# Values of two heads in one product of 512 columns, and a new order of heads and projections

## The chip, the core and the metric

The kernel runs on one core of one Trainium2 chip. The metric is the device time of one execution in microseconds. The kernel before took 1372.91 us (median of three runs, 1370.94 to 1373.17).

A core has TensorE (PE in the profile, with the loads of its stationary operand shown apart as PEld), VectorE (DVE), ScalarE (ACT) and GpSimd (POOL). SyncE (SP) and POOL issue the DMAs here. Each engine executes its own instructions in the order in which they were issued to it, and waits at an instruction until what that instruction needs is there. TensorE multiplies into PSUM, which has eight banks of 128 x 512 float32. VectorE and ScalarE read and write PSUM and SBUF.

## The reference

One decoder layer on 1024 tokens of 1024 features, all in float32. The part that the change touches is the retention mixer:

```python
h = rmsnorm(x, ln_mix)
z = h @ w_in                       # q | k | v | gate | pool | branch gates
qh = rotary(q) * dk ** -0.5        # 4 heads of 128
kh = rotary(k)
vh = v                             # 4 heads of 256
ret = retention_chunkwise(qh, kh, vh)
```

`retention_chunkwise` cuts the tokens into eight chunks of 128. In each chunk and head it takes decayed scores of q and k times v, and adds q times a running state. The state is 128 x 256 per head and goes from chunk to chunk: decay times the state before, plus k transposed times v of the chunk. After it come a norm per head, a gate, an output projection, a pooling mixer, gated mixing, and an MLP with squared relu. The result must agree with this in float32, so each matrix operand is carried as a pair of reduced-precision parts, an upper and a lower, and each product is three: upper by upper, upper by lower, lower by upper (`PASSES`).

## The kernel before

Activations lie feature-major in `hT[k][half]`: for each of eight blocks k of 128 features and each half of 512 tokens, a tile with the upper and the lower part. The stages follow one another: load and scale x, retention by heads, the pool input (`pool_input`, tiles `pu` and `u`), blocks for a Strassen-like scheme (`mixed_blocks`, tiles `xw` and `hx`), twelve mixer units (`ps_Xmx` and so on), output projections, and the MLP.

In the retention stage `rotary` makes q or k of a head: 24 products of 512 columns for each half of the tokens (the weight is stationary, `hT` moves), then four VectorE steps. `values(h)` makes v of one head, tokens by features: `hT` is stationary (128 tokens), and the weight of the head moves with its 256 columns, 24 products for each of eight token tiles; two token tiles share a PSUM bank. v is split into upper and lower parts (`split_scaled`, ScalarE and then VectorE) and stays in SBUF until `retain(h)`.

`retain(h)` is a chain over all four engines. Keys are transposed (`ps_kt`), scaled and split (`kz`). Scores (`ps_s`) are masked in place and split (`scm`). q is split (`qp`). For each chunk `ps_kv` is k times v, `st` the new state (a VectorE step that reads the state before), and `sp` its split. `ps_ret` adds scores times v and q times state. Then `rn` is copied, its statistics taken (`bst`, `mv`, `rs`, `nb`), and normalised. `transposed` turns it (`ps_rt`), and `retn` goes to DRAM.

PSUM has two pools: five banks "mm" for projections and values, three banks "aux" for `retain` and `transposed`. SBUF tiles are rings by tag. The tag "raw" has two buffers of 4 KB a partition: `load_raw` loads each 512 KB piece of a weight into one, and the piece is split into a `w_` tile from there. A new user of a buffer waits until the one before has been read.

The kernel is written stage by stage, but a scheduler sets the order on each engine when the program is built. It goes by its own estimates of durations, prefers what was written earlier, and puts an instruction where it believes that its inputs are ready; work written later fills the gaps of a chain. On the chip that order is fixed.

## Time and profile before

| | before |
|---|---|
| time, median of three runs | 1372.91 us |
| profiled execution | 1370.83 us, span 1369.0 us |
| granted TensorE clock, mean | 0.997 |
| TensorE busy | 1353.6 us, 99% of the span |
| VectorE, ScalarE busy | 987.9 us (72%), 565.1 us (41%) |
| value products | 41.7 to 224.6 us of the span, 768 of 256 columns |
| first mixer unit's first product | 285.07 us |

A row of the profile names the line of the kernel, engine, operation, tile written and tiles read, the shape, the count, busy time and mean duration, and the idle time of the engine just before with what ended it. Matmuls are pipelined: the duration of one is longer than the distance to the next, and the pace is read from starts. A window row gives the stretch in us, its length, busy us and count of instructions of each engine, and at its end the granted TensorE clock, the DMA share and GB/s; a window with a filter counts only the instructions that the filter leaves. In the list of DMA issues stand the bytes of one transfer and the median time from its issue to its landing.

### The profile page before, as it was taken

How to read it: one execution, taken by the hardware profiler on the slowest of the kernel's cores; microseconds unless marked ns; L12 is line 12 of the kernel's file. 1: busy time of each engine (PE TensorE's matmuls, PEld its weight loads, DVE VectorE, ACT ScalarE, POOL GpSimd, SP SyncE). 2: the span in 40 equal slices, each digit the busy share in tenths (PEclk: the TensorE clock that was granted, in tenths of full speed). 3: DMA queues.
4: the chain of work that ended last, by engine and by line, in shares of the span. 5: the costliest groups of instructions: out<-in, count | busy, mean ns of one | idle time of the engine just before them, and what ended most of it. 6: DMA issues, size and time to landing. Idle time of an engine off the chain costs nothing. (4 is left out here: it accounts for less than half of the span.)

```text
span 1369.0 us, 17491 instructions
## 1 busy us (share of the span) xinstructions
PE 1353.6 (99%) x6572; PEld 1138.6 (83%) x6572; DVE 987.9 (72%) x1631; ACT 565.1 (41%) x960; POOL 86.1 (6%) x151
## 2 busy tenths in 40 slices
PE   9999999999999999999999999999999999999997
PEld 6998999878888888888887888888888888888886
DVE  5766565789966768628657878777787977689665
ACT  6234425463334344113445433333333544444372
POOL 0000001111000000000001011101111000000000
PEclk9999999999999999999999999999999999999999
DMA  9122021354342367124422344433437989778423
GB/s 360 50 62 77 17 92 63 124 215 158 121 172 85 112 238 261 62 77 170 154 77 77 116 169 169 151 126 147 169 139 292 407 330 351 261 266 307 159 70 123
DMA packets 65444, 225.07 MB, mean 164 GB/s; under 512 B 7376, under 2 KB 9424, under 8 KB 61264
## 3 DMA queue, kind: packets, MB, share of 16 engines
q1 hardware_dynamic: 47152, 158.66, 32.7%
q0 software_dynamic: 17920, 65.02, 12.5%
q8 instruction: 51, 0.84, 0.3%
q10 hardware_dynamic: 288, 0.29, 0.1%
q14 instruction: 33, 0.27, 0.1%
HBM read 167.31 MB, written 56.62 MB: 164 GB/s over the span
## 5 line engine op out<-in xcount | busy, mean ns | idle before, releaser
L121 PE MATMUL ps_v<-w_v_hi,hT 128*128 128x256 f32 x512 | 96.0, 284 | 0.0
L199 PE MATMUL ps_Xup<-mv,w_up 128*128 128x512 f32 x384 | 93.0, 390 | 1.7 <-DVE w_up L135 1.7
L199 PE MATMUL ps_Zup<-mv,w_up 128*128 128x512 f32 x384 | 92.5, 389 | 0.8 <-ACT w_up L134 0.8
L853 PE MATMUL ps_dnX<-db,da 128*128 128x512 f32 x384 | 93.1, 389 | 0.1
L134 ACT ACTIVATE w_up<-raw_up 128x512 fp32r<-128x512 f32 x96 | 58.3, 627 | 84.4 <-DVE raw_up L192 46.3
L199 PE MATMUL ps_Vup<-mv,w_up 128*128 128x512 f32 x384 | 92.6, 389 | 0.0
L121 PE MATMUL ps_yr<-retT,w_ret 128*128 128x512 f32 x384 | 88.5, 389 | 0.5 <-ACT w_ret L94 0.5
L121 PE MATMUL ps_o<-mixT,w_o 128*128 128x512 f32 x384 | 87.5, 389 | 0.0
L199 PEld LDWEIGHTS ps_Xup<-mv,w_up 128*128 128x128 f32 x384 | 71.9, 188 | 16.9 <-DVE w_up L135 2.1
L121 PEld LDWEIGHTS ps_yr<-retT,w_ret 128*128 128x128 f32 x384 | 72.0, 188 | 15.8 <-ACT w_ret L94 0.9
L199 PEld LDWEIGHTS ps_Zup<-mv,w_up 128*128 128x128 f32 x384 | 72.0, 188 | 15.7 <-ACT w_up L134 0.8
L853 PEld LDWEIGHTS ps_dnX<-db,da 128*128 128x128 f32 x384 | 72.0, 188 | 15.5 <-DVE db L135 0.5
L199 PEld LDWEIGHTS ps_Vup<-mv,w_up 128*128 128x128 f32 x384 | 72.0, 188 | 15.1 <-ACT w_up L134 0.2
L121 PEld LDWEIGHTS ps_o<-mixT,w_o 128*128 128x128 f32 x384 | 72.0, 188 | 15.0
L135 DVE TENSOR_TENSOR w_up<-raw_up,w_up 128x512 fp32r<-128x512 f32 x96 | 64.2, 685 | 26.4 <-ACT w_up L134 26.1
L121 PEld LDWEIGHTS ps_v<-w_v_hi,hT 128*128 128x128 f32 x512 | 80.8, 192 | 0.0
L134 ACT ACTIVATE w_mx<-raw_mx 128x512 fp32r<-128x512 f32 x72 | 43.6, 626 | 86.0 <-DVE raw_mx L192 44.0
L121 PE MATMUL ps_v<-w_v_lo,hT 128*128 128x256 f32 x256 | 72.6, 284 | 0.0
L199 PE MATMUL ps_Xmx<-hT,w_mx 128*128 128x512 f32 x288 | 72.0, 396 | 0.3 <-ACT w_mx L134 0.3
L199 PE MATMUL ps_Vmx<-hx,w_mx 128*128 128x512 f32 x288 | 69.5, 389 | 0.0
L728 ACT ACTIVATE act<-act 128x512 f32<-128x512 f32 x64 | 40.3, 629 | 65.6 <-DVE act L727 62.2
L199 PEld LDWEIGHTS ps_Xmx<-hT,w_mx 128*128 128x128 f32 x288 | 55.1, 192 | 12.5 <-ACT w_mx L134 0.6
(249 smaller groups left out, 2819.9 us busy)
## 6 DMA issues: line engine op xcount, KB each, us to landing
act_dram<-act POOLq DMA_DIRECT2D x48, 512.0 KB, 4.7
ad<-act_dram SPq DMA_DIRECT2D x48, 512.0 KB, 6.6
raw_up<-in_w_up_dram SPq DMA_DIRECT2D x16, 1024.0 KB, 5.0
raw_mx<-in_w_mix_dram SPq DMA_DIRECT2D x12, 1024.0 KB, 6.2
sg_dram<-mx POOLq DMA_DIRECT2D x16, 512.0 KB, 4.7
wa_lo<-in_w_down_dram SPq DMA_DIRECT2D x16, 512.0 KB, 9.0
wb_hi<-in_w_down_dram SPq DMA_DIRECT2D x16, 512.0 KB, 7.5
wc_lo<-in_w_down_dram SPq DMA_DIRECT2D x16, 512.0 KB, 4.3
```

The costliest lines, as they stand in the source:

```text
L121: nc.tensor.matmul(ps, stationary(k, sa), moving(k, sb), start=i == 0, stop=i == n - 1)
L134: nc.scalar.activation(dst[:, 0, :], src, AF.Copy)
L135: nc.vector.tensor_tensor(dst[:, 1, :], src, dst[:, 0, :].bitcast(F32), ALU.subtract)
L199: nc.tensor.matmul(ps, ws[x][:, sa, k * P : (k + 1) * P], moving[x][k][:, sb, :], start=start and k == 0 and n == 0, stop=k == 3 and n == ...
L728: nc.scalar.activation(dst, dst, AF.Square)
L853: nc.tensor.matmul(banks[i][:, c0 : c0 + n], w[:, sa, i * P : (i + 1) * P], x[:, sb, c0 : c0 + n], start=start and j == 0 and m == 0, stop ...
```

## The change

`values` now makes two heads at once: the moving operand is 512 columns wide, 256 of head h and 256 of head h + 1, and each token tile fills one PSUM bank. The weight of a pair comes in four pieces of 512 KB (`value_weights`): two are split into `w_` tiles, two into four tiles of the tag "a".

In the first call (heads 0 and 1) the values of head 0 are split as before; those of head 1 are scaled by ScalarE into a tile `vf` of the tag "raw" and written to DRAM by the POOL queue. In the second call (heads 2 and 3) both heads go to DRAM that way. `stored_values(h)` loads them back (`vs`) and splits them. The three heads' values are written and read once, 1 MB each way per head.

The order in which the work is written changes too: the second call's weights are asked for before `retain(0)`, its products come after head 1's `retain` and `transposed`, q and k of head 2 follow these, and q and k of head 3 come after head 2's. Nothing else is computed differently.

```diff
-    def load_wide(src, name, raws=None):
-        whi, wlo = w_tile(name + "_hi"), w_tile(name + "_lo")
-        for i in range(2):
-            sl = slice(i * S, (i + 1) * S)
-            raw = raws[i] if raws else load_raw(src[i], f"{name}_{i}")
-            split_weights(raw, whi[:, sl], wlo[:, sl])
-        return [w.rearrange("p (k j) -> p k j", j=256) for w in (whi, wlo)]
...
-    raw_v = [load_raw(a["w_v"][0][0], "w_v0_0")]
-    raw_v.append(load_raw(a["w_v"][0][1], "w_v0_1"))
+    raw_v = [load_raw(a["w_v"][0][i], f"w_v0_{i}") for i in range(4)]
...
-    def values(h):
-        w = load_wide(a["w_v"][h], f"w_v{h}", raw_v if h == 0 else None)
+    v_dram = dram_tile("v_dram", (NH, P, TT, DV))
+
+    def value_weights(h, raws=None):
+        ws = []
+        for i in range(4):
+            raw = raws[i] if raws else load_raw(a["w_v"][h // 2][i], f"w_v{h}_{i}")
+            if i < 2:
+                w = w_tile(f"w_v{h}_{i}").rearrange("p (s n) -> p s n", s=2)
+                split_weights(raw, w[:, 0, :], w[:, 1, :])
+                ws += [w[:, :, :HALF], w[:, :, HALF:]]
+            else:
+                for j in range(2):
+                    w = pair_tile("a", f"w_v{h}_{i}_{j}")
+                    split_pair(w, raw[:, j * HALF : (j + 1) * HALF])
+                    ws.append(w)
+        return ws
+
+    def values(h, ws, direct=None):
+
+        for t in range(TT):
+            half = t // 4
+            ps = mm_bank(f"ps_v{h}_{t}")
+            c0 = t % 4 * P
+            product(
+                ps, KT,
+                lambda k, s: hT[k][half][:, s, c0 : c0 + P],
+                lambda k, s: ws[k][:, s, :],
+            )
+            scale = rstd1[half][:, t % 4 : t % 4 + 1]
+            if direct is None:
+                f = rpool.tile([P, 2, DV], F32, tag="raw", name=f"vf{h}_{t}")
+                nc.scalar.activation(f.rearrange("p h e -> p (h e)"), ps, AF.Copy, scale=scale)
+                nc.gpsimd.dma_start(v_dram[h : h + 2, :, t, :].rearrange("h p e -> p h e"), f)
+                continue
+            if t % 2 == 0:
+                direct.append(a_tile("r", f"v{h}_{t // 2}", F32R, (P, 2, 2, DV)))
+            split_scaled(direct[-1][:, :, t % 2, :], ps[:, :DV], scale)
+            f = rpool.tile([P, DV], F32, tag="raw", name=f"vf{h}_{t}")
+            nc.scalar.activation(f, ps[:, DV:], AF.Copy, scale=scale)
+            nc.gpsimd.dma_start(v_dram[h + 1, :, t, :], f)
+        return direct
+
+    def stored_values(h):
         v = []
         for pr in range(TT // 2):
...
+            if pr % 2 == 0:
+                f = a_tile("r", f"vs{h}_{pr}", shape=(P, 4, DV))
+                nc.sync.dma_start(f, v_dram[h, :, 2 * pr : 2 * pr + 4, :])
+            v.append(a_tile("r", f"v{h}_{pr}", F32R, (P, 2, 2, DV)))
+            split_pair(
+                v[pr].rearrange("p s i e -> p s (i e)"),
+                f[:, pr % 2 * 2 : pr % 2 * 2 + 2, :].rearrange("p i e -> p (i e)"),
+            )
         return v
...
-    v[0] = values(0)
+    v[0] = values(0, value_weights(0, raw_v), [])
     for h in range(NH):
         n = h + 1
-        if n < NH:
-            if n > 1:
-                (q[n],) = rotary((n, f"qT{n}"))
-            (k[n],) = rotary((NH + n, f"kT{n}"))
+        if h:
+            v[h] = stored_values(h)
+        if h == 0:
+            (k[1],) = rotary((NH + 1, "kT1"))
+            w_v = value_weights(2)
         rn = retain(h, q[h], k[h], v[h])
         if n < NH:
             transposed(h, rn)
-        if n < NH:
-            v[n] = values(n)
+        if h == 1:
+            values(2, w_v)
+            q[2], k[2] = rotary((2, "qT2"), (NH + 2, "kT2"))
+        if h == 2:
+            q[3], k[3] = rotary((3, "qT3"), (NH + 3, "kT3"))
```

The order in which the engines are issued their work shows three places that the prediction speaks of. A trailing number in a name tells tiles of one kind apart, and the digits before it are the head and the piece.

The first is SP's queue of weight loads. Before, behind the second piece of head 0's value weight:

```order
L87 DMA raw_w_v0_1_155<-in_w_v_dram 128x1024
L87 DMA raw_w_kT1_658<-in_w_fm_dram 128x1024
L87 DMA raw_w_v1_0_939<-in_w_v_dram 128x1024
L87 DMA raw_w_v1_1_943<-in_w_v_dram 128x1024
L87 DMA raw_w_qT2_1164<-in_w_fm_dram 128x1024
```

Now:

```order
L87 DMA raw_w_v0_1_155<-in_w_v_dram 128x1024
L87 DMA raw_w_v0_2_157<-in_w_v_dram 128x1024
L87 DMA raw_w_v0_3_159<-in_w_v_dram 128x1024
L87 DMA raw_w_kT1_703<-in_w_fm_dram 128x1024
L87 DMA raw_w_v2_0_768<-in_w_v_dram 128x1024
```

The load of head 1's key weight (`raw_w_kT1`) moved behind two more value pieces, and by the ring "raw" also behind the eight tiles `vf0_0` to `vf0_7`: its buffer is the one that `vf0_6` used.

The second is VectorE in head 1's `retain`. Before, from the second half of q's split:

```order
L135 TENSOR_TENSOR qp1_1_1330<-qT1_374,qp1_1_1330 128x512
L135 TENSOR_TENSOR sp1_0_1337<-st1_1335,sp1_0_1337 128x256
L420 SCALAR_TENSOR_TENSOR st1_1335<-st1_1335,ps_kv1_0_1336 128x256
L420 SCALAR_TENSOR_TENSOR st1_1335<-st1_1335,ps_kv1_1_1350 128x256
L135 TENSOR_TENSOR sp1_0_1337<-st1_1335,sp1_0_1337 128x256
L420 SCALAR_TENSOR_TENSOR st1_1335<-st1_1335,ps_kv1_1_1350 128x256
```

Now, from the third state:

```order
L445 SCALAR_TENSOR_TENSOR st1_1064<-st1_1064,ps_kv1_1_1079 128x256
L95 TENSOR_TENSOR w_qT2_1462<-raw_w_qT2_1463,w_qT2_1462 128x1024
L127 TENSOR_TENSOR sp1_0_1066<-st1_1064,sp1_0_1066 128x256
L127 TENSOR_TENSOR sp1_1_1080<-st1_1064,sp1_1_1080 128x256
L445 SCALAR_TENSOR_TENSOR st1_1064<-st1_1064,ps_kv1_1_1079 128x256
L95 TENSOR_TENSOR w_kT2_1468<-raw_w_kT2_1469,w_kT2_1468 128x1024
L445 SCALAR_TENSOR_TENSOR st1_1064<-st1_1064,ps_kv1_2_1093 128x256
L127 TENSOR_TENSOR sp1_1_1080<-st1_1064,sp1_1_1080 128x256
L127 TENSOR_TENSOR sp1_2_1094<-st1_1064,sp1_2_1094 128x256
L95 TENSOR_TENSOR w_qT3_1824<-raw_w_qT3_1825,w_qT3_1824 128x1024
L95 TENSOR_TENSOR w_kT3_1830<-raw_w_kT3_1831,w_kT3_1830 128x1024
L445 SCALAR_TENSOR_TENSOR st1_1064<-st1_1064,ps_kv1_2_1093 128x256
```

The lower halves of four weights (`w_qT2`, `w_kT2`, `w_qT3`, `w_kT3`), which stood outside this chain, now stand between its states.

The third is TensorE in head 3's `retain`. Before, from the second scores:

```order
L387 MATMUL ps_s3_1_2332<-qT3_1740,kT3_1806 128x128 x4
L121 MATMUL ps_pu0_1_2526<-hT6_1_210,w_pu0_2494 128x512 x3
L121 MATMUL ps_pu0_1_2526<-hT7_1_213,w_pu0_2494 128x512 x3
L366 MATMUL ps_kv3_0_2348<-v3_0_2091,kz3_0_2312 128x256 x3
L366 MATMUL ps_kv3_1_2362<-v3_1_2145,kz3_0_2312 128x256 x3
L121 MATMUL ps_pu1_0_2559<-hT0_0_163,w_pu1_2553 128x512 x3
```

Now, from the last product of `pu2_0`, the fifth of the eight `pu` banks:

```order
L113 MATMUL ps_pu2_0_2303<-hT7_0_193,w_pu2_2297 128x512 x3
L494 MATMUL ps_rt2_1_1_1817<-ident_92,rn2_1_1747 128x128 x4
L403 MATMUL ps_kt3_0_1972<-ident_92,kT3_1835 128x128 x4
L412 MATMUL ps_s3_0_1980<-qT3_1829,kT3_1835 128x128 x4
L403 MATMUL ps_kt3_1_1989<-ident_92,kT3_1835 128x128 x4
L412 MATMUL ps_s3_1_1997<-qT3_1829,kT3_1835 128x128 x4
L391 MATMUL ps_kv3_0_2013<-v3_0_1958,kz3_0_1977 128x256 x3
L391 MATMUL ps_kv3_1_2027<-v3_1_1961,kz3_0_1977 128x256 x3
L391 MATMUL ps_kv3_2_2041<-v3_2_1966,kz3_1_1994 128x256 x3
```

and on to the last `ps_ret3` with nothing between; the sixth `pu` product follows it. On VectorE the first copy of a `pu` bank (`u0`) stands behind the last split of head 3's states:

```order
L127 TENSOR_TENSOR sp3_3_2056<-st3_2012,sp3_3_2056 128x256
L127 TENSOR_TENSOR hx3_0_2282<-xw0_2277,hx3_0_2282 128x512
L127 TENSOR_TENSOR hx5_0_2286<-xw0_2277,hx5_0_2286 128x512
L533 TENSOR_TENSOR u0_2164<-ps_pu0_0_2165,R1_130 128x512
L533 TENSOR_TENSOR u0_2164<-ps_pu0_1_2191,R1_130 128x512
```

Four and a half `pu` products that stood inside head 3's chain now stand ahead of it.

More of the change, by code (lines that the diff above doesn't have):

```diff
@@ L344, in values @@
+    def stored_values(h):
         v = []
         for pr in range(TT // 2):
-            vt = a_tile("r", f"v{h}_{pr}", F32R, (P, 2, 2, DV))
-            ps = mm_bank(f"ps_v{h}_{pr}")
-            half = pr // 2
-            for i in range(2):
-                c0 = (pr % 2 * 2 + i) * P
-                product(
-                    ps[:, i * DV : (i + 1) * DV], KT,
-                    lambda k, s: hT[k][half][:, s, c0 : c0 + P],
-                    lambda k, s: w[s][:, k, :],
-                )
@@ L356, in values @@
-            for i in range(2):
-                t = pr % 2 * 2 + i
-                split_scaled(
-                    vt[:, :, i, :], ps[:, i * DV : (i + 1) * DV], rstd1[half][:, t : t + 1]
-                )
-            v.append(vt)
+            if pr % 2 == 0:
[6 more added lines that the diff above has]
+            )
@@ L1021, in _wide @@
 def _wide(w):
-    n = w.shape[1] // 256
+    n = w.shape[1] // HALF
     return np.ascontiguousarray(
-        w.reshape(2, 4, P, n, 256).transpose(3, 0, 2, 1, 4).reshape(n, 2, P, S)
+        w.reshape(4, 2, P, n, HALF).transpose(3, 0, 2, 1, 4).reshape(n, 4, P, S)
     )
```

## The prediction

> **What bounds the kernel now.** I read the page's head first, then the groups of instructions by line, then the order of time on TensorE.
>
> ```profile
> span 1369.0 us, 17491 instructions
> PE 1353.6 (99%) x6572; PEld 1138.6 (83%) x6572; DVE 987.9 (72%) x1631; ACT 565.1 (41%) x960; POOL 86.1 (6%) x151
> L121 PE MATMUL ps_v<-w_v_hi,hT 128*128 128x256 f32 x512 | 96.0, 284 | 0.0
> L121 PE MATMUL ps_v<-w_v_lo,hT 128*128 128x256 f32 x256 | 72.6, 284 | 0.0
> L121 PEld LDWEIGHTS ps_v<-w_v_hi,hT 128*128 128x128 f32 x512 | 80.8, 192 | 0.0
> ```
>
> TensorE is busy 99% of the span and the 768 value products wait for nothing. So time changes only by TensorE's own work getting shorter, or by TensorE waiting where it did not. Mean durations (284 ns) overlap; the pace is read from starts:
>
> ```profile
> 30.70 11.18 PE L121 MATMUL ps_qT<-hT,w_qT 128*128 128x512 f32 x48
> 41.72 0.28 PE L121 MATMUL ps_v<-w_v_hi,hT 128*128 128x256 f32 x1
> 50.55 0.40 PE L121 MATMUL ps_v<-w_v_hi,hT 128*128 128x256 f32 x2
> 50.79 0.28 PE L121 MATMUL ps_v<-w_v_lo,hT 128*128 128x256 f32 x1
> 50.91 0.40 PE L121 MATMUL ps_v<-w_v_hi,hT 128*128 128x256 f32 x2
> 50.00:60.00 10.00, 10.00 (x85) 10.00 (x85) 1.84 (x4) 1.31 (x3) 1.00 0.00 1
> ```
>
> Three products of 256 columns take 0.36 us (50.55 to 50.91), 0.120 each; the ten-microsecond window, of the value products' instructions alone, holds 85 of them (its columns are stretch, length, then busy us and count of PE, PEld, DVE, ACT). 48 products of 512 columns take 11.02 us (30.70 to 41.72), 0.2296 each.
>
> **What the change removes.** 768 products of 256 columns become 384 of 512; every other count on TensorE stays. 768 x 0.120 = 92.2 us against 384 x 0.2296 = 88.2 us: **-4.0 us**. That is the whole gain, because a wide product costs nearly two narrow ones.
>
> **What it adds: three places where the issued order leaves TensorE with nothing to do.** TensorE executes in order, so each is a sum of waits.
>
> *First: weights behind a store.* The copies vf go through the two "raw" buffers that weights are loaded into. The key weight of head 1 used to be loaded during the first value products; now its buffer is that of vf0_6, so it waits for product 6, the copy, the store, the load and the split, and only product 7 and one transpose group cover that.
>
> ```profile
> 39.70 0.33 SPq L87 DMA_DIRECT2D raw_w_kT<-in_w_fm_dram  x1
> 43.50 1.06 ACT L94 ACTIVATE w_kT<-raw_w_kT 128x1024 fp32r<-128x1024 f32 x1 [6.45 <-DMA raw_w_kT<-in_w_fm_dram]
> 44.60 1.23 DVE L95 TENSOR_TENSOR w_kT<-raw_w_kT,w_kT 128x1024 fp32r<-128x1024 f32 x1
> L138 ACT ACTIVATE v<-ps_v,rstd_a 128x256 fp32r<-128x256 f32 x32 | 14.2, 474 | 21.5 <-DVE v L139 9.2 <-PE ps_v L121 8.4 <-PE ps_ret L366 2.0
> retn_dram<-retn POOLq DMA_DIRECT2D x8, 512.0 KB, 3.5
> out_dram<-o SPq DMA_DIRECT2D x8, 256.0 KB, 2.5
> u_dram<-u POOLq DMA_DIRECT2D x4, 512.0 KB, 6.2
> ```
>
> From the end of product 6: two ScalarE copies 0.95; the store of 128 KB, which the trace lacks, between 2.5 (256 KB) and 6.2 (512 KB), taken as 3.0 since it is the smallest; the load 3.8 (39.70 to 43.50); the split 1.06; four hand-overs of some 0.1, an estimate from gaps such as 44.56 to 44.60. Sum 9.2. Cover: 24 x 0.2296 + 0.36 = 5.9. Wait 3.3, and 0.3 more for the lower half (1.23 against four products). **+3.6**, bounds 2.8 (store 2.5, load 3.5) to 8 (6.2 and 5.1, the row of raw_w_qT below).
>
> The clock then matters:
>
> ```profile
> 281.00:285.00 4.00, 2.79 (x17) 1.69 (x15) 3.27 (x6) 4.00 (x10) 0.54 (x1) 1.00 0.98 356
> 285.00:290.00 5.00, 4.93 (x13) 3.65 (x14) 2.63 (x5) 3.71 (x9) 1.06 (x2) 0.66 0.99 403
> 285.07 4.87 PE L199 MATMUL ps_Xmx<-hT,w_mx 128*128 128x512 f32 x12 [0.34 <-ACT w_mx L134]
> 289.78 0.62 PE L199 MATMUL ps_Ymx<-hx,w_mx 128*128 128x512 f32 x2
> ```
>
> After 4 us of transposes with gaps TensorE was granted 0.66 of its clock (next to last but two column) in 285 to 290, and 12 products took 4.71 instead of 2.76 us. I charge this once, behind the longest wait: **+2.0**, bounds 0 and 4 (twice).
>
> The Trainium skill's "TensorE: Matmul & The Clock Gate", Part 1, says that the clock halves after an idle window of about 3.4 us and returns after as long a busy one. By its rule the first wait (3.3 us and a transpose group) may or may not be caught, and the short waits below would be free; by the row a broken 4 us is enough. With the rule the term is 0 or about 1.7 us, an estimate from that page; the sum would move by less than its bounds.
>
> At the start the weights of products k = 4 to 7 arrive through the same two buffers, and the half for k = 6 is ready about 0.9 us after its product could start (an estimate from VectorE's queue around 44.60 above): **+0.9**, bounds 0 and 2.
>
> *Second: head 1's recurrence behind weight splits.* There the lower halves of four weights stand on VectorE between the states. w_kT2 needs the store of vf2_7, and w_kT3 the buffer of w_kT2; both splits stand ahead of state 5. From head 1's first transpose: last value product 5.1 (24 us-work: 0.36 x 2 + 0.8 + 16 x 0.23), copy 0.8, a store of 256 KB taken at retn's 3.5, load 4.2, splits 1.06 + 1.23, second load 4.2, splits 2.3, giving 22.7 with hand-overs; then states 5 and 6, statistics, three rotary steps and the last split, 4.2: 26.9, and the last two products end at 27.3. TensorE's own work up to there, by the paces quoted above and below, is 24.6. **+2.7**; with a store of 2.5 and loads of 3.5 it is 0.3, with 6.2 and 5.1 it is 7.
>
> ```profile
> raw_w_v<-in_w_v_dram SPq DMA_DIRECT2D x8, 512.0 KB, 4.2
> raw_w_qT<-in_w_fm_dram SPq DMA_DIRECT2D x3, 512.0 KB, 5.1
> ```
>
> *Third: head 3 with nothing beside it.* Before, products of pu fill the gaps of head 3's chain:
>
> ```profile
> 233.68 0.60 PE L378 MATMUL ps_kt<-ident,kT 128*128 128x128 f32 x4
> 234.04 3.69 PE L121 MATMUL ps_pu<-hT,w_pu 128*128 128x512 f32 x15
> 237.57 1.05 PE L387 MATMUL ps_s<-qT,kT 128*128 128x128 f32 x8
> 238.37 1.62 PE L121 MATMUL ps_pu<-hT,w_pu 128*128 128x512 f32 x6
> 239.83 0.88 PE L366 MATMUL ps_kv<-v,kz 128*128 128x256 f32 x6
> 240.54 4.72 PE L121 MATMUL ps_pu<-hT,w_pu 128*128 128x512 f32 x20
> 263.44 0.52 PE L366 MATMUL ps_ret<-v,scm 128*128 128x256 f32 x3
> 263.80 0.52 PE L366 MATMUL ps_ret<-sp,qp 128*128 128x256 f32 x3
> ```
>
> Now five pu products fill all five "mm" banks beforehand, the sixth needs the copy u0, and u0 stands on VectorE behind the last state's split. TensorE's own work from kt3_0 to that product: 2 x 0.36 + 2 x 0.8 + (21 + 45) x 0.12 = 10.2 us. The chain, at VectorE's paces:
>
> ```profile
> 263.81 3.07 DVE L504 TENSOR_TENSOR u<-ps_pu,R 128x512 f32<-128x512 f32 x5
> L420 DVE SCALAR_TENSOR_TENSOR st<-st,ps_kv 128x256 f32<-128x256 f32 x24 | 10.1, 420 | 18.0 <-PE ps_kv L366 17.4
> L135 DVE TENSOR_TENSOR sp<-st,sp 128x256 fp32r<-128x256 f32 x28 | 11.6, 418 | 6.4 <-ACT sp L134 6.0
> L139 DVE SCALAR_TENSOR_TENSOR kz<-ps_kt,decays,kz 128x512 fp32r<-128x512 f32 x8 | 5.9, 743 | 0.0
> L446 DVE BATCH_NORM_STATS2 bst<-rn 128x6 f32<-128x256 f32 x32 | 11.7, 413 | 1.3 <-ACT rn L442 1.2
> L138 ACT ACTIVATE kz<-ps_kt,decays 128x512 fp32r<-128x512 f32 x8 | 5.4, 676 | 0.0
> ```
>
> ScalarE frees from the transposes before at 0.9 and splits kz to 1.6, VectorE to 2.3; the second scores wait for that bank ("aux" has three) and end at 3.4; masks, scm, kz, scm and qp, six 512-wide steps of 0.6 to 0.66 (u's five took 3.0), to 6.5; then the states alternate with their splits, 0.34 to 0.42 each, with three waits for a bank: state 2 at 8.5, state 4 at 10.1, state 5 at 11.9 behind ps_kv3_2, statistics, state 6, last split 13.9. The output products go at 11.7, 13.1 and 14.5 and end at 16.0. **+5.8**. Below: VectorE's queue alone is 10.5 us from 1.6, and 0.7 of products follow: 12.8 - 10.2 = 2.6. Above: half as much again, 9.
>
> *What lies beside.*
>
> ```profile
> 100.00:125.00 25.00, 25.00 (x159) 22.32 (x158) 14.47 (x38) 13.99 (x26) 3.27 (x4) 1.00 0.24 85
> ```
>
> VectorE splits 12 tiles of 512 columns in place of 24 of 256, 12 x 0.6 against 24 x 0.4 at u's and st's paces: no more. ScalarE makes 16 more copies of at most 0.6, some 10 us over the 200 us of this stage, of which a stretch such as 100 to 125 leaves it 11 of 25 us free (VectorE 10.5). POOL issues 16 stores; SP 6 loads of stored values, tens of microseconds ahead of their use. All at nothing; a stored value that came late would cost its load, 4 to 5 us.
>
> **Sum.** -4.0 + 3.6 + 2.0 + 0.9 + 2.7 + 5.8 = +11.0 us. The profiled execution took 1370.8 us (span 1369.0 and 1.8 around it), so 1381.8 like for like; it lies 2.1 below the median of the runs shown, 1372.9, which gives 1383.9. I forecast **1383**.
>
> **Rivals.**
> *The order covers itself (faster).* The waits above are ones the scheduler's order already avoids or the queues absorb, so that the narrow products' overhead is all that moves: 1372.9 - 4.0 = 1369. For it: before, TensorE's waits came to almost nothing though the same kind of order was issued. Against it: five full banks and u0 behind head 3 are not a matter of timing. It decides where the three waits together fall below 4 us, while their lower bounds are 2.8 + 0.3 + 2.6 = 5.7.
> *A draw.* Waits near those bounds, no clock loss: -4.0 + 5.7 = +1.7, about 1375.
> *Loads of the stationary operand set the pace (far faster).* PEld is busy 10.00 of 10 us above, one load 192 ns long; were its 192 ns the pace, 768 x 0.192 - 384 x 0.23 would save 59 us: 1314. The count of 85 products in that window contradicts it. The Trainium skill's "Trainium Kernel Development and Optimization", Best Practices, tells the reader to judge by LDWEIGHTS busy rather than matmul busy, which would point this way; here the starts decide.
> *The waits compound (slower still).* Each buffer wait at its upper bound and two clock losses: -4.0 + 8 + 4 + 2 + 7 + 9 = +26, 1399.
>
> **How the numbers follow.** Forecast (slower by some 4 to 23 us, 1377 to 1396) 0.72; compounding 0.08; draw 0.10, of which a little reaches into slower; covered 0.08; loads 0.02. A change of 0.2%, 2.7 us, is about what can be told from none. Faster 0.10, same 0.09, slower 0.81. The range takes in the forecast and the draw's upper part and most of the bounds: 1372 to 1397.
>
> **What would show it.** Right: TensorE waits of 3 us or more before ps_kT of head 1, released by ScalarE's w_kT and a landed load; waits in ps_ret, ps_kv and before ps_pu of some 6 us in head 3; a granted clock below 1 behind the first. ps_v at 0.23 us a product. Wrong: no wait before ps_kT of head 1, or head 3's stretch in less than 13 us, or a value stage that shrinks by more than 5 us.

## The result and the profile after

The changed kernel took **1389.46 us** (median of three runs, 1388.76 to 1389.59) against 1372.91: 1.0125 times the time before, 95% interval 1.0108 to 1.0142. It is slower by 17 us; 1383 was forecast.

The profiled execution lasted 1389.59 us, its span 1387.5, against 1370.83 and 1369.0. The head of its page:

```profile
span 1387.5 us, 16792 instructions
PE 1360.2 (98%) x6188; PEld 1125.0 (81%) x6188; DVE 984.4 (71%) x1623; ACT 571.8 (41%) x968; POOL 96.1 (7%) x167
PEclk9999999889999999999999999999999999999999
```

TensorE has 384 instructions fewer, yet is busy for 6.6 us longer: a product that runs at a lower granted clock is busy for longer (the 48 products of `ps_kT` below take 12.64 us in place of 11.0). The clock's row has digits of 8 in the eighth and ninth of its 40 slices. All but 0.7 us of the loss lies ahead of the mixer's first product (`ps_Xmx`), which began at 285.07 us before and begins at 302.91 now, 17.8 later. What follows takes 1084.6 us against 1083.9.

The order of time on TensorE, at the places that the prediction named (start, length, the product, count, the wait ahead of it):

```profile
48.23 0.96 PE L113 MATMUL ps_v<-w_v,hT 128*128 128x512 f32 x3 [0.30 <-DVE w_v L127]
49.65 2.56 PE L113 MATMUL ps_v<-w_v,hT 128*128 128x512 f32 x10 [0.46 <-DVE rot_qT L329]
...
91.83 12.80 PE L113 MATMUL ps_kT<-hT,w_kT 128*128 128x512 f32 x48 [2.91 <-ACT w_kT L94]
104.47 1.75 PE L113 MATMUL ps_v<-w_v,hT 128*128 128x512 f32 x7
...
162.78 0.62 PE L391 MATMUL ps_kv<-v,kz 128*128 128x256 f32 x3 [0.40 <-DVE st L443]
167.15 5.29 PE L113 MATMUL ps_qT<-hT,w_qT 128*128 128x512 f32 x22 [0.52 <-DVE w_qT L95]
...
257.89 0.60 PE L403 MATMUL ps_kt<-ident,kT 128*128 128x128 f32 x4
260.11 1.16 PE L412 MATMUL ps_s<-qT,kT 128*128 128x128 f32 x8 [0.28 <-DVE kz L131]
262.74 3.10 PE L391 MATMUL ps_kv<-v,kz 128*128 128x256 f32 x12 [1.47 <-DVE scm L127]
266.36 1.65 PE L391 MATMUL ps_kv<-v,kz 128*128 128x256 f32 x6 [0.51 <-DVE st L445]
268.52 1.65 PE L391 MATMUL ps_ret<-v,scm 128*128 128x256 f32 x6 [0.51 <-DVE st L445]
276.62 16.51 PE L113 MATMUL ps_pu<-hT,w_pu 128*128 128x512 f32 x72
...
296.43 0.33 PE L494 MATMUL ps_rt<-ident,rn 128*128 128x128 f32 x1 [3.30 <-ACT rn L481]
301.91 1.11 PE L494 MATMUL ps_rt<-ident,rn 128*128 128x128 f32 x4 [1.55 <-ACT retn L497]
302.91 5.02 PE L191 MATMUL ps_Xmx<-hT,w_mx 128*128 128x512 f32 x12
```

The three places are there: the wait for head 1's key weight (2.91 us, released by ScalarE's split as foretold, with 48 products at a lower clock behind it: 12.64 us from start to start in place of 11.0), short waits in head 1, and head 3 with nothing beside it from 257.89 to 276.62. A fourth was not foretold: the entry to the mixer, where the last `pu` product is over at 293 us and the transposes of head 3's result come in pieces.

Three stretches of it by windows (stretch, length, then busy us and count of PE, PEld, DVE, ACT and POOL, granted clock, DMA share, GB/s):

```profile
257.90:276.60 18.70, 15.87 (x92) 14.40 (x91) 14.17 (x31) 10.77 (x22) 0.54 (x1) 0.73 0.15 57
276.60:293.00 16.40, 16.40 (x74) 13.35 (x72) 11.96 (x32) 5.42 (x9) 7.25 (x11) 1.00 0.89 319
293.00:302.90 9.90, 4.78 (x17) 2.89 (x16) 8.18 (x15) 9.90 (x19) 0.54 (x1) 0.70 0.61 230
```

Head 3's chain runs at a clock of 0.73, and the entry at 0.70 with TensorE busy for less than half of it while ScalarE is busy throughout. ScalarE's own order of time in the entry shows with what:

```profile
292.65 2.19 ACT L541 ACTIVATE xw<-xw,vec 128x1024 f32<-128x1024 f32 x2 [4.69 <-DMA xw<-in_xT_dram]
...
295.79 4.03 ACT L481 ACTIVATE rn<-rn,nb,rs 128x256 f32<-128x256 f32 x8
```

The eight steps that normalise head 3's `rn` stand in ScalarE's queue behind the scaling of the last mixer block `xw3`, and that waits 4.69 us for its load. POOL issued that load, once a `pu` product had set its buffer free, at 282.55, and it landed 10 us later:

```profile
282.55 0.72 POOL L538 DMA_DIRECT2D xw<-in_xT_dram  x1 [2.15 <-PE ps_pu L113]
```

Before, the stretch from the last `pu` product (281.0) to `ps_Xmx` took 4.07 us; now it takes 9.9. The normalisation stood behind `xw3` there too, and as many `pu` products (72) lay behind head 3's chain. The load of `xw3` makes the difference. Its issue and its scaling before:

```profile
268.38 0.71 POOL L509 DMA_DIRECT2D xw<-in_xT_dram  x1 [1.25 <-DVE hx L135]
274.81 2.19 ACT L512 ACTIVATE xw<-xw,vec 128x1024 f32<-128x1024 f32 x2 [1.63 <-DMA xw<-in_xT_dram]
```

Head 3's chain ended at 264.2 us before and ends at 276.6 now. Counted from there, the load is now issued 1.7 us later and takes 3.7 us longer (10.1 in place of 6.4). These 5.4 us are the whole by which the way from the chain's end to `ps_Xmx` grew (20.9 us before, 26.3 now). The load of the block ahead of it was issued 1.2 us ahead of the chain's end before (262.99), and is issued 3.1 us behind it now (279.68), so the two lie closer together. That this is why the last load takes longer was not tested by itself.

### The profile page after: what moved, and what is told of

It reads as the page before. It is cut to its first block, busy times and chain, and to the rows that moved or that the text cites. A ratio compares the mean times of both kernels' runs of the same rounds, so it can differ in the third digit from the quotient of the medians.

```text
span 1387.5 us, 16792 instructions
## 1 busy us (share of the span) xinstructions
PE 1360.2 (98%) x6188; PEld 1125.0 (81%) x6188; DVE 984.4 (71%) x1623; ACT 571.8 (41%) x968; POOL 96.1 (7%) x167
## 5 line engine op out<-in xcount | busy, mean ns | idle before, releaser
L113 PE MATMUL ps_v<-w_v,hT 128*128 128x512 f32 x384 | 91.3, 393 | 0.8 <-DVE rot_qT L329 0.5
L113 PEld LDWEIGHTS ps_v<-w_v,hT 128*128 128x128 f32 x384 | 70.9, 188 | 15.9 <-DVE rot_qT L329 0.9
L191 PEld LDWEIGHTS ps_Vmx<-hx,w_mx 128*128 128x128 f32 x288 | 54.1, 188 | 11.2
```

Of the source, the lines that this page charges most:

```text
L113: nc.tensor.matmul(ps, stationary(k, sa), moving(k, sb), start=i == 0, stop=i == n - 1)
L191: nc.tensor.matmul(ps, ws[x][:, sa, k * P : (k + 1) * P], moving[x][k][:, sb, :], start=start and k == 0 and n == 0, stop=k == 3 and n == ...
```

## The experiments

Each kernel was timed beside the kernel before. Differences to the changed kernel are worked out from the two ratios and 1371 us, which the kernel before took in these comparisons; each ratio's interval is about ±2 us, so a difference of two kernels is known to about ±3 us. A profile shows one execution of its kernel, and not the median. Unless said otherwise the edit is to the changed kernel.

### 1. The key weight of head 1 loaded early

```diff
-    v[0] = values(0, value_weights(0, raw_v), [])
+    w_v = value_weights(0, raw_v)
+    w_first["kT1"] = load_piece(a["w_fm"][NH + 1], "w_kT1")
+    v[0] = values(0, w_v, [])
```

> Theory (three stalls in the issued order, as the trace of the changed kernel reads): 1384.8 us. The key weight of head 1 is asked for ahead of the first value products, so it no longer needs the buffer of vf0_6; the wait of 2.9 us ahead of ps_kT of head 1 goes, and with it the 1.8 us that its 48 products took longer at a granted clock of 0.72. The 48 products take 11.0 us again. Rival (the storage itself costs: stores, loads and copies beside the products): the wait moves to the next tile that needs a raw buffer, and the time stays at 1389.

Measured: 1383.56 us, 1.0095 (1.008 to 1.011), 4.1 us less than the changed kernel. Its TensorE:

```profile
88.65 11.04 PE L113 MATMUL ps_kT<-hT,w_kT 128*128 128x512 f32 x48
99.53 0.60 PE L403 MATMUL ps_kt<-ident,kT 128*128 128x128 f32 x4
```

The wait is gone and the 48 products take 10.9 us. So the first place cost the wait of 2.9 and 1.6 of clock, as a cause and not only as a row beside a loss.

The run told something else by the way. Head 3's chain is untouched by the edit, and its instructions stand in the same order. Yet it ran at full clock (a window of this kernel):

```profile
253.40:269.80 16.40, 12.72 (x93) 11.12 (x92) 13.58 (x30) 10.37 (x21) 0.55 (x1) 1.00 0.17 65
```

16.3 us from the first transpose to the first `pu` product behind the chain, in place of 18.7. So 2.4 of head 3's cost is clock, and the chain itself is 16.3. The profile is of the shortest of this kernel's four executions (1382.79 to 1385.40 us).

### 2. Each wide product as two of 256 columns

```diff
-            product(
-                ps, KT,
...
-                lambda k, s: ws[k][:, s, :],
-            )
+            for e in range(2):
+                product(
+                    ps[:, e * DV : (e + 1) * DV], KT,
...
+                    lambda k, s: ws[k][:, s, e * DV : (e + 1) * DV],
+                )
```

> Each value product of 512 columns is issued as two of 256, all else of the changed kernel stays. Theory (a wide product costs nearly two narrow ones, 0.2296 against 2 x 0.120): 4.0 us more, 1393.5, and ps_v at 0.120 a product. Rival one (loads of the stationary operand set the pace, 192 ns each): 59 us more. Rival two (the stalls absorb it): 1389.

Measured: 1401.07 us, 1.0221 (1.0205 to 1.0236), 13.2 more than the changed kernel, where 4.0, 59 or nothing were expected. The paces, from windows of the value products alone (columns to PE's count, then clock, DMA share, GB/s), of this kernel and then of the changed one:

```profile
50.00:55.00 5.00, 4.52 (x21) 0.50 0.01 3
55.00:60.00 5.00, 5.00 (x37) 0.83 0.00 0
60.00:78.00 18.00, 18.00 (x152) 1.00 0.09 30
```

```profile
52.00:88.00 36.00, 36.00 (x160) 1.00 0.08 26
```

With the end of the last one added, a narrow product takes 0.120 us ((18 + 0.28)/152), a wide one 0.227 ((36 + 0.39)/160), as the theory had it. 384 wide ones are 87.3 us and 768 narrow ones 92.2: **width is worth about 4.9 us**. Of the other 8.3 us, about 6 are an effect of the edit that I had not thought of: the first half of a product now goes through all eight blocks k in 2.9 us, where the wide one took 5.5, so the weights' late pieces keep TensorE waiting three times (0.94, 1.18 and 1.40 us in place of 0.30 and 0.46), and the clock stands at 0.50 and 0.83 for the next ten microseconds. The remaining 2 are assigned to no place. It is no clean measurement of the width by its total, only by its pace.

### 3. Is it that head 1 begins late? One pair, or the order, undone

The first split of a head's keys (`kz`) came at 78.63 us before and comes at 105.30 now, 26.7 later, and head 3 begins 26.7 later too (231.19 and 257.89, while some `pu` products went ahead). A tempting theory: the late start of the recurrence leaves head 3 alone at the end. Experiment 5 undoes heads 0 and 1 (narrow values as before, no store; the weights of heads 2 and 3 stay wide); 6 undoes heads 2 and 3 with their order; 7 is 6 with the edit of experiment 1; 8 keeps all values wide and puts the projections back where they stood.

The edit of experiment 5 (`narrow_values` and its weights are the kernel's before):

```diff
-    v[0] = values(0, value_weights(0, raw_v), [])
+    v[0] = narrow_values(0)
...
-        if h:
+        if h > 1:
             v[h] = stored_values(h)
...
-            w_v = value_weights(2)
...
+        if h == 0:
+            v[1] = narrow_values(1)
+            w_v = value_weights(2)
```

> Heads 0 and 1 as in the kernel before (two products of 256 columns, each head's beside the chain of the head ahead of it, nothing stored), heads 2 and 3 still in one product and through DRAM, with the changed order. Theory (late start: the four heads' chains run back to back from head 0's scaled keys kz0, which the first pair pushed from 78.6 to 105.3 us, and everything behind moved with it): kz0 is back at 79 and the first mixer product near 286, 1372 us. Rival (the second pair: v3's products no longer stand beside head 2's chain, products of pu take their place there, and head 3 is left bare wherever the chain starts): the first wait and its clock go (4.7 us), head 3's 16 to 19 us and the late entry stay, 1384.

Measured: 1386.4 us, 1.0117 (1.0103 to 1.0131). Its TensorE:

```profile
169.97 0.73 PE L121 MATMUL ps_qT<-hT,w_qT 128*128 128x512 f32 x2 [1.77 <-ACT w_qT L94]
302.71 5.06 PE L199 MATMUL ps_Xmx<-hT,w_mx 128*128 128x512 f32 x12
```

The recurrence begins where it began before the change (`kz` at 78.92 us), and the mixer still begins at 302.7, where the late-start theory had 286. As the explanation of the whole that theory falls; the time lies near the rival's 1384. Without the first place's loss there is a new wait at head 2's query weight (1.77 us, 0.53 more behind it, and a clock of 0.5 to 0.65 at 170 to 178 us); head 3 and the entry are as in the changed kernel (a wait of 3.59 us for `rn`).

The edit of experiment 6:

```diff
-        if h:
+        if h == 1:
             v[h] = stored_values(h)
...
-            w_v = value_weights(2)
+        if n in (2, 3):
+            (q[n],) = rotary((n, f"qT{n}"))
+            (k[n],) = rotary((NH + n, f"kT{n}"))
...
-        if h == 1:
-            values(2, w_v)
-            q[2], k[2] = rotary((2, "qT2"), (NH + 2, "kT2"))
-        if h == 2:
-            q[3], k[3] = rotary((3, "qT3"), (NH + 3, "kT3"))
+        if n in (2, 3):
+            v[n] = narrow_values(n)
```

> Heads 0 and 1 in one product, head 1's values through DRAM, as in the changed kernel; heads 2 and 3 as in the kernel before, with their order of q, k and values. Theory (late start of head 0's chain decides): kz0 stays at about 105 and the first mixer product near 300, 1387 us. Rival (second pair): products of pu stand in head 3's chain again, the first mixer product near 288, and only the first wait with its clock, the start and half the width stay: 1372.9 + 2.9 + 1.8 + 0.8 - 2.0 = 1376.

Measured: 1384.24 us, 1.0101 (1.0086 to 1.0117).

```profile
144.72 0.58 PE L121 MATMUL ps_v<-w_v_hi,hT 128*128 128x256 f32 x1 [3.21 <-DVE rot_qT L337]
```

Head 3 has 87 `pu` products beside it again, and its chain takes 30.8 us with them, only about 0.6 more than TensorE's own work there (87 x 0.2296 + 10.2); in the changed kernel it was 8.5 more. So head 3's loss comes from the second half of the change. But the first place's loss remains, and a wait of 3.21 us stands in the middle, where head 2's values wait for VectorE's rotary steps; TensorE had no such wait before. Both expectations missed: the time and the first mixer product (297.94) lie nearer to the late start's 1387 and 300 than to the rival's 1376 and 288.

Experiment 7 adds the early key weight to that.

> The kernel of the second pair undone, and besides the key weight of head 1 asked for ahead of the first value products. Late start decides: about 6 us less than without that, 1381, as kz0 moves up by 6. Second pair decides: 1376 less the first wait and its clock, 4.7: 1371.6, the same as the kernel before or faster by the half of the width.

Measured: 1379.92 us, 1.0064 (1.0051 to 1.0076), 5.1 less than experiment 6, about what experiment 1 gained. Of the variants of the changed kernel that compute everything it takes the least time, and it is slower than the kernel before. It, too, lies nearer to what the late start gave (1381) than to the rival's 1371.6. So a late start does not explain the loss by itself (experiment 5), but 6 and 7 don't exclude that it has a share.

The edit of experiment 8:

```diff
+        if n in (2, 3):
+            (q[n],) = rotary((n, f"qT{n}"))
+            (k[n],) = rotary((NH + n, f"kT{n}"))
...
-            q[2], k[2] = rotary((2, "qT2"), (NH + 2, "kT2"))
-        if h == 2:
-            q[3], k[3] = rotary((3, "qT3"), (NH + 3, "kT3"))
```

> Both pairs in products of 512 columns through DRAM; only the order of the projections is put back: q and k of head 2 ahead of head 1's retain, q and k of head 3 ahead of head 2's. The waits of 1.7 us in head 1 behind weight splits should go; head 3 is still issued without a product of pu beside it. Theory (cover of head 3, which the order of q and k does not give back): 1387. Rival (the order of q and k is what costs): 1376 or less.

Measured: 1401.29 us, 1.0221 (1.0207 to 1.0235), 13 us more than the changed kernel: a miss for both expectations. The values' new place with the projections' old one is the worst of these orders; for head 2's query weight alone TensorE waits 3.96 us:

```profile
109.08 7.13 PE L113 MATMUL ps_qT<-hT,w_qT 128*128 128x512 f32 x22 [3.96 <-ACT w_qT L94]
```

What follows: the two halves of the change cost 16.0 us (only heads 2 and 3 changed, experiment 5) and 13.9 (only heads 0 and 1, experiment 6), both together 17.1. The costs do not add. Each of these orders has broken places of its own.

### 4. Head 3's chain and the entry to the mixer

The prediction put head 3's cost down to the `pu` products having all gone ahead of it. Before, some 99 of the 192 single products, a little over four banks' worth, stood inside its chain. Experiment 2 writes the pool input's first group ahead of `retain(3)`. The scheduler then puts some 49 `pu` products inside the chain again.

```diff
+        if h == 3:
+            for g in range(1):
+                pool_input(g)
         rn = retain(h, q[h], k[h], v[h])
```

> Theory: 1375 us. The first pool input is written ahead of head 3's retain, so its copies u0 free two mm banks and products of pu2 and pu3 stand inside head 3's chain again. Head 3's 18.7 us shrink by about 8.5 (waits and clock), and the block xw3, no longer behind a late pu2, lands early, so that the 5.8 us of the entry to the mixer units go too. Rival one (the entry is late for another reason, the end of head 3's chain): only the first part goes, 1381. Rival two (the chain of head 3 only moves and ends the stage later): 1389.

Measured: 1393.25 us, 1.0163 (1.0147 to 1.0178), 5.2 more. Every expectation missed. Its TensorE, then its ScalarE, then its VectorE:

```profile
283.43 5.63 PE L113 MATMUL ps_pu<-hT,w_pu 128*128 128x512 f32 x24
295.99 1.95 PE L494 MATMUL ps_rt<-ident,rn 128*128 128x128 f32 x4 [6.93 <-ACT rn L481]
300.40 3.07 PE L494 MATMUL ps_rt<-ident,rn 128*128 128x128 f32 x12 [2.46 <-ACT rn L481]
303.36 4.53 PE L191 MATMUL ps_Xmx<-hT,w_mx 128*128 128x512 f32 x12
```

```profile
295.34 2.08 ACT L481 ACTIVATE rn<-rn,nb,rs 128x256 f32<-128x256 f32 x4 [6.48 <-DVE nb L479]
```

```profile
288.64 3.09 DVE L127 TENSOR_TENSOR hx<-xw,hx 128x512 fp32r<-128x512 f32 x5
291.65 0.74 DVE L471 BATCH_NORM_STATS2 bst<-rn 128x6 f32<-128x256 f32 x2
```

Inside the chain the filler removed about half of the loss (25.8 us with 49 products beside it, where TensorE's own work is 21.5), and only 24 products were left behind it. The wait went to the entry, 6.93 and 2.46 us. The first half of `rn` waits for statistics on VectorE that stand behind splits of mixer blocks. The second half waits for the last steps of its statistics, which stand behind a step that waits 2.38 us for the mixer's weights:

```profile
297.90 0.69 DVE L184 TENSOR_TENSOR tmp_mx<-raw_mx 128x512 f32<-128x512 f32 x1 [2.38 <-DMA raw_mx<-in_w_mix_dram]
```

From head 3's first transpose to `ps_Xmx` this kernel takes 45.7 us, the changed one 45.0. In this kernel, then, what counted was the **whole chain from head 3's keys to the first mixer product**, and moving TensorE's own work along it gained nothing.

Experiment 3 takes away the block that stands ahead of `rn` in ScalarE's queue: the scale of `xw3` is read from a copy that VectorE makes out of `rn` (times zero, plus the scale), so that its scaling must be issued behind `rn`.

```diff
-    mixed_blocks(3)
+    gain3 = stat.tile([P, 2], F32, tag="gain3", name="gain3", bufs=1)
+    for i in range(2):
+        f = V_LNM + 3 + 4 * i
+        nc.vector.scalar_tensor_tensor(
+            gain3[:, i : i + 1], rn[i][:, 3, :1], 0.0, vec[:, f : f + 1], ALU.mult, ALU.add
+        )
+    mixed_blocks(3, gain3)
```

> Head 3's chain stays as it is; the scaling of block xw3 takes its factor from two small VectorE steps that read the normalised rows of head 3 (times zero), so ScalarE normalises first. Theory (ScalarE stood at the late xw3 load with the normalisation behind it): the wait of 3.3 us ahead of ps_rt and most of the 5.8 us at the entry go, first mixer product at 298 instead of 302.9, 1385 us. Rival (xw3 itself is what is late, and the mixer's first product with its blocks waits for it instead): the same time, 1389, with the wait in ps_Ymx.

Measured: 1385.22 us, 1.0099 (1.0079 to 1.0118), 3.6 less and close to the 1385 that was expected.

```profile
278.83 16.51 PE L113 MATMUL ps_pu<-hT,w_pu 128*128 128x512 f32 x72
...
298.41 0.65 PE L494 MATMUL ps_rt<-ident,rn 128*128 128x128 f32 x4 [0.67 <-ACT retn L497]
300.45 5.49 PE L191 MATMUL ps_Xmx<-hT,w_mx 128*128 128x512 f32 x12 [1.38 <-ACT w_mx L126]
```

The entry's waits fall from 3.30 and 1.55 us to 0.67 and 1.38. From the end of head 3's chain (278.83) to `ps_Xmx` it is 21.6 us, in place of 26.3 in the changed kernel and 20.9 before. That shows the normalisation's place behind `xw3` as the cause of 4.7 of the 5.4 us by which this way grew.

The first mixer product came at 300.45 and not at the 298 that was expected, in the main because this execution lost more clock ahead of it: head 1's 48 key products, which the edit doesn't touch, took 13.9 us and not 12.64, and head 3's chain 19.2 and not 18.7. It is the longest of this kernel's four executions, which took 1382.5 to 1388.12 us at mean clocks of 0.996 to 0.989.

Experiment 11 takes all of the mixer's blocks away (loads, scaling, sums, splits), with one tile of zeros in their place; TensorE's products stay, the mixer's results are not the reference's.

```diff
     def mixed_blocks(k):
-        xw = w_tile(f"xw{k}", F32).rearrange("p (i t) -> p i t", i=2)
-        nc.gpsimd.dma_start(xw, a["xT"].rearrange("(i k p) t -> k p i t", i=2, p=P)[k])
...
+        for t in (T1, T3, T2, T4):
+            hx[t][k] = zero
```

> The blocks for the mixer (their 4 loads of 1 MB, 16 sums on VectorE, and 16 splits on ScalarE and VectorE) are left out, and one tile of zeros stands in for all 16; TensorE's order is the same. So the mixer's results are not the reference's; what is read is the time from head 3's first transpose to the first mixer product, 45.0 us in the changed kernel. Theory (head 3's chain itself is short enough, the work on blocks beside it and ahead of its normalisation makes the entry late): head 3's part stays at 16 to 19 us, the 72 products 16.5, the entry falls from 9.9 to about 4 us: first mixer product 5 to 8 us earlier, 1381. Rival (the chain is too long for 72 products to cover, blocks or not): the entry stays at 8 us or more, 1387.

Measured: 1378.44 us, 1.0066 (1.0049 to 1.0083), 8.1 less. By its windows, at the first and the third of the stretches above:

```profile
258.30:274.70 16.40, 12.72 (x93) 11.11 (x92) 13.36 (x32) 8.70 (x17) 1.49 (x2) 1.00 0.10 39
291.00:293.80 2.80, 1.98 (x17) 1.65 (x15) 1.99 (x4) 2.13 (x5) 1.08 (x2) 1.00 0.91 317
```

Without that work on ScalarE and VectorE the entry takes 2.8 us in place of 9.9; head 3's chain is as long as in experiment 1 and at full clock. So the entry's loss hangs on the blocks: their loads, and their work in the queues. The run takes both away at once and doesn't tell them apart.

Experiment 12 makes experiment 3's edit to the kernel before.

> The kernel before, unchanged but for the edit that lets ScalarE normalise head 3 ahead of the mixer's last block. There the normalisation ran from 278.5 to 283.0 us behind the scaling and three splits of that block (3.9 us of ScalarE), the 72 products of pu ended at 281.0, and the first mixer product came at 285.07 with a granted clock of 0.66 behind it. Theory (the same order costs at this place in the kernel before, only less): normalised by about 281, first mixer product at 283, and perhaps the 2 us of clock: 2 to 4 us less, 1368. Rival (the last block, now 4 us later, is what the mixer's products then wait for): no gain or some us more, 1371 to 1374.

Measured: 1370.48 us beside 1370.93, 0.9996 (0.9986 to 1.0005): no change, where 2 to 4 us of gain were expected. Its first mixer product begins at 284.86 us, against 285.07. There `rn` is normalised sooner, but `xw3`'s scaling then stands ahead of the copies of `retn`, and TensorE waits 1.35 us for these. Its first 12 mixer products ran at full clock (3.29 us in place of 4.87), and even that doesn't show in the time. In the old order the normalisation stood behind `xw3` as well, but the load came earlier (ScalarE waited 1.63 us for it, not 4.69), and there was little to repair.

### 5. Is it the clock or the wait? Products that compute nothing, and all repairs together

Experiment 9 fills three waits with products whose results nobody reads: 12 of 512 columns ahead of head 1's keys, 14 ahead of the last transposes, 10 of 128 columns in the last gap.

```diff
+    def busy(ps, n):
+        for i in range(n):
+            nc.tensor.matmul(
+                ps, hT[0][0][:, 0, :P], hT[0][0][:, 0, :], start=True, stop=True
+            )
...
+            if name == "kT1" and half == 0:
+                busy(ps, 12)
```

> The changed kernel with products that compute nothing, put where TensorE waits: 12 of 512 columns ahead of head 1's first key product, 14 ahead of head 3's last transposes and 10 of 128 columns in the gap before the last four. All waits stay as they are. Theory (a broken stretch also halves the granted clock behind it, and that is a cost of its own): head 1's 48 key products take 11.0 us in place of 12.6 (-1.8), the transposes and the first 12 products of the mixer run at full clock (-1 and -2.2): about 4 to 5 us less, 1384.5. Rival (the clock follows something else than TensorE's own gaps): the same time, 1389.

Measured: 1389.55 us, 1.0137 (1.0123 to 1.0152), no gain over the changed kernel.

```profile
92.30 11.53 PE L113 MATMUL ps_kT<-hT,w_kT 128*128 128x512 f32 x48 [0.22 <-ACT w_kT L94]
```

```profile
298.46 1.95 PE L506 MATMUL ps_rt<-ident,rn 128*128 128x128 f32 x8 [0.17 <-ACT rn L493]
300.20 3.66 PE L322 MATMUL ps_busy<-rn 128*128 128x128 f32 x20
304.06 3.27 PE L191 MATMUL ps_Xmx<-hT,w_mx 128*128 128x512 f32 x12
```

At the first place it went as the clock theory says: TensorE kept busy through the wait, the 48 products behind it take 11.4 us to the next start in place of 12.64. In the entry it failed. The clock stood at 0.72, 0.50, 0.50 and 0.57 in the four microseconds from 299 us on, although TensorE was busy then, first with transposes and then with the ten late products (20 instructions). Ahead of that the filler had ended too early: TensorE still waited 0.77 us ahead of the first transpose and some 0.16 us ahead of each of the next four. The late products ran slowly, and `ps_Xmx` began 1.1 us later than in the changed kernel. What was won at `ps_Xmx` (12 products in 3.27 us, not 5.02) was lost ahead of it.

Experiment 10 puts 1 and 3 together, with five of the late products.

> The changed kernel with head 1's key weight asked for ahead of the value products, ScalarE normalising head 3 ahead of the last block, and 5 idle products of 128 columns in the last gap. Theory (these are separate costs): 4.1 + 3.6 us as measured apart, and a little for the clock: 1379 on the scale where the changed kernel is 1388 and the kernel before 1371. Rival (one wait takes the place of the other): 1383 or more.

Measured: 1382.01 us, 1.008 (1.0068 to 1.0093), 6.2 less than the changed kernel, where 1 and 3 alone gave 4.1 and 3.6. The expectation was 1379 if the costs are separate, and 1383 or more if one takes the place of the other; with these intervals the run doesn't tell the two apart. In the profiled execution (1379.59 us, the shortest of five) the clock was full from 40 to 298 us:

```profile
270.24 16.51 PE L113 MATMUL ps_pu<-hT,w_pu 128*128 128x512 f32 x72
...
291.88 3.29 PE L191 MATMUL ps_Xmx<-hT,w_mx 128*128 128x512 f32 x12 [1.16 <-ACT w_mx L126]
```

From the end of head 3's chain to `ps_Xmx` it is 21.6 us again, where experiment 1, without the edit of experiment 3, has 26.6. With both large faults mended the change still loses 11 us on the kernel before: head 3's bare chain and the smaller places are left.

## Why the prediction was right and where it failed

The sign, the size within its range and the mechanism (the issued order leaves TensorE with nothing to do) held. The sum was 7.8 us short of the profiled execution. Against the profiled execution of before, up to the first mixer product:

| term | predicted | measured |
|---|---|---|
| width of the value products | -4.0 | -4.9 |
| start: weight pieces late | +0.9 | +0.8 |
| first wait | +3.6 | +2.9 |
| clock behind it | +2.0 | +1.6 |
| head 1's recurrence | +2.7 | +1.7 |
| head 3 with nothing beside it | +5.8 | +8.5 |
| entry to the mixer | not priced | +5.8 |
| sum | +11.0 | +16.4 of 17.8 |

The terms that were priced come to +10.6 in this execution, close to the +11.0. That closeness is in part luck: width, start, first wait, clock and head 1 all came out lower, and head 3's lost clock, which was not foreseen there, made up for them.

**Width.** Right in kind: a wide product costs nearly two narrow ones. Its pace is 0.227 us, and not the 0.2296 taken from projections; 384 times the difference is nearly the 0.9 by which the term was short. The rival that judged by the loads of the stationary operand (1314) is out.

**First place.** Cause, releaser and size were right, and experiment 1 shows the cause (4.1 us back, 4.5 by the rows). The wait of 2.91 us is just below the 3 that was named as the sign. The wait was 0.7 shorter than worked out: the store of 128 KB, taken at 3.0 us, lands in a median of 2.2.

**Clock, charged once.** The first place's 1.6 was in the bounds. That it would come only behind the longest wait was wrong: it fell again in head 3 and in the entry. The 1.6 is one execution's: the same 48 products took from 12.5 to 13.9 us in the profiles of experiments 2, 3, 4, 6 and 11, so the clock cost 1.5 to 2.9 there.

**Head 1.** About the size (0.40, 0.50, 0.25 and 0.52 us at 162.8 to 167.2), but not as described: four short waits along the chain and at the projection behind it, and none before the last two products, where the prediction had it.

**Head 3.** The chain was worked out at 16.0 us from VectorE's paces, and at full clock it is 16.3 (experiments 1, 10 and 11). This is the part that the method did best. The term came to 8.5 only because the changed kernel's execution ran it at 0.73 of the clock, 2.4 us more. Of the signs that were named, some 6 us of waits did not show as such: the waits in the chain's rows come to 2.8 us (3.6 in experiment 1), no wait stands ahead of `ps_pu`, and the rest is a slower pace between them. Experiment 6 shows that the chain loses only about 0.6 us where `pu` products stand beside it in the old order. As a remedy for the new order the filler did not do: with it back (experiment 2), a loss of the same size stood at the entry.

**The step that failed** is the sentence that ended "What lies beside": "All at nothing". It looked at ScalarE's and VectorE's load along the value stage and at nothing behind head 3's last output products. But the chain goes on: statistics, normalisation, transposes, copies, and only then can `ps_Xmx` begin. The 72 `pu` products behind it left 4.1 us of this uncovered before, and 9.9 now: the last block `xw3`, behind which `rn` stands in ScalarE's queue, is scaled 16.0 us after the chain's end and not 10.6. That cost 5.8 us, most of what the sum was short by. Experiment 3 shows it (the stretch from the chain's end to `ps_Xmx` falls from 26.3 to 21.6 us; 3.6 back in the time), experiment 10 repeats it (21.6), and with no blocks at all it is 19.1 (experiment 11).

**What stays open.** 1.4 of the 17.8 us are assigned to no place (1.8 if one counts that a gap of 0.4 us between head 3's chain and the `pu` products, there before, is gone); waits under 0.3 us that were not counted are the nearest candidates. What lies behind the mixer's first product takes from 1082.7 to 1086.6 us in the profiles of kernels that do the same there. Why the load of `xw3` took longer was not tested, and head 1's short waits were changed by no experiment alone. And it was not settled what decides whether head 3's chain loses its clock.

## What to carry to other kernels

Where one engine is busy 99% of the time, price a re-ordering by the whole chain up to the first instruction of the next stage, and ask what work is still there to cover it; a filler that is moved into a chain is missing behind it. Walk through the queue of every engine on that chain, as issued: an instruction that waits for a load ahead of the chain's next step can hold the whole chain back (here 4.69 us of waiting, and the repair shortened the way to the mixer's first product by 4.7). A narrow gain from each instruction (here 4.9 us for half as many products) is soon outweighed: the two repaired places gave about 4 us each, each half of the change alone cost nearly as much as the whole (16.0 and 13.9 us against 17.1), and the costs of the parts did not add up to the whole's.

## What was unexpected of the hardware

**The same instructions with the same waits, at two clocks.** In head 3 the kernel after and experiment 1 have the same rows up to the wait of 1.47 us for `scm`. The windows just ahead of and behind that wait (length, PE busy and count, clock, DMA share, GB/s), of after and of experiment 1:

```profile
261.90:263.90 2.00, 1.16 (x5) 0.75 0.01 4
263.90:265.90 2.00, 1.95 (x9) 0.50 0.00 0
```

```profile
257.45:259.45 2.00, 1.08 (x6) 1.00 0.00 0
259.45:261.45 2.00, 1.30 (x7) 1.00 0.00 0
```

TensorE was granted half its clock in the one and all of it in the other, after a like share of work. The chain took 18.7 us after the change, 19.2 and 18.1 in experiments 3 and 9, and 16.3 in experiments 1, 10 and 11. The Trainium skill's "TensorE: Matmul & The Clock Gate", Part 1 ("What's actually happening"), says that activity is watched in a free-running window of about 3.4 us, and that the moment at which the clock changes at a kernel's start depends on where in that window the first matmul lands. The two clocks for one row of instructions would agree with the same holding for pauses in mid-kernel; no run here moved the chain against such a window alone, so it is not shown to be the cause.

**A pause filled with transposes and small products: two outcomes.** In experiment 9 TensorE was busy from 298.46 us on with transposes and then products of 128 columns, and the clock fell to 0.50. The same page's Part 4 says that a transpose doesn't count as busy in the same way. This case doesn't settle it: in experiment 10 the same kinds of instructions, half as many of the small products, stood at the same place with a wait of 1.16 us behind them, and the clock stayed at 1.00 from 284 to 298 us. Ahead of the fall in experiment 9 stood waits of 1.4 us in all within 2.8 us, and they may be its cause as well.

**Small stores are quick and a large load can be slow.** The trace's list of DMA issues has medians of 2.2 us for the stores of 128 KB and 2.6 for those of 256 KB, where 3.0 and 3.5 were taken. The last block's load of 1 MB took 10 us, while the median of the four is 5.7, in a stretch in which 0.89 of the DMA engines' time was taken.
